# Forming the weight operands of the first two gate/up units earlier, and keeping one unit's operands for both token pairs

## The chip, the cores and the metric

The kernel runs on one NeuronCore of a Trainium2 chip. The core has a matrix engine (TensorE, PE in the profile; its weight loads are the row PEld), VectorE (DVE), ScalarE (ACT), GpSimd (POOL), and SyncE (SP), which issues nearly all DMAs of this kernel, in order. The metric is the device time of one execution in microseconds, smaller is better. Time before is the median of three runs.

## The reference

One layer of a streaming encoder for 1088 tokens (1024 of a prompt, 64 of a running stream) with 1024 channels, all in 32-bit floats. The part that the change touches is the end of the mixer and the start of the feed-forward network:

```python
    x = x + ym @ w_out                      # output projection, 1024 x 1024
    h = rmsnorm(x, g_ffn)
    x = x + (jax.nn.silu(h @ w_gate) * (h @ w_up)) @ w_down      # D_FF = 2816
```

The outputs are the two normalised results and small state tensors.

## The kernel before

**Precision.** A product of 32-bit matrices is made of three passes of TensorE in its rounded 32-bit type: both factors are split into a rounded part (suffix h) and the rest (suffix l), and the passes are h·h, h·l and l·h. ScalarE makes h by a cast, VectorE makes l by a subtraction.

**Gate and up.** The 2816 gate and up columns are worked off in 22 units `j` of 128 gate and 128 up columns (`NF`). The 1088 tokens form two pairs, x = 0 and x = 1, each of two quarters of 272 tokens (`Q`). A unit multiplies a 2x2 block matrix of weights by a 2x2 block matrix of tokens with seven products instead of eight. So there are seven token operands per pair (`R0[c]`, `R1[c]`, named B11, T1, T2, B21, T3, B22, T4 in the order of use, each with h and l) and seven weight operands per unit. A product is 4 (channel tiles) x 3 (passes) = 12 matmuls of 272 columns for one pair, so a unit has 84 matmuls for one pair and 168 for both.

**Weight operands.** `load_w` (L609 to L617) fetches four weight blocks into three slots F (three DMAs on SP). `steps` (L619 on) forms the seven operands in four steps; each step ends in `put`, which takes a slot pair from `w_free`, casts F to h on ScalarE (L627) and subtracts on VectorE (L471). Three pairs hold two operands (128x1024), the fourth holds one (128x512). `fill()` takes steps as long as slot pairs are free; `products` calls it ahead of each product, and gives a pair back (`give`) when both of its operands were used. Slots: F starts with three `raws` tiles; from unit 2 on it has also the tiles R, E and C, ten in all. W has three `ring` pairs, and from unit 2 on a fourth in the tile Hl67.

**PSUM.** A unit adds its seven products up in three accumulators (banks a, b, c) of four buffers. ScalarE copies partial results out (`grab`, L693: p1, p5, u2, u3), VectorE adds (L474) and multiplies (L719, L720) the rest. Bank b is free after the addition of p2 (at B21), bank c after that of p53 (at B22), bank a after the multiplication at T4. The next product into a bank that holds a copied partial result waits for that copy.

**Order of the stages.** The output projection runs over 8 column blocks `m` for x = 0 and then again for x = 1. Its weights, split in the first round, are written to DRAM (`wod`) and reloaded (`reload`) in the second. `out_evac` adds the residual (L474) and ScalarE squares it (L535, L541, L544). After a round come the row sums of squares (`stat`: 1-column matmuls L484, then L489 and POOL's L491), a transposed row (`row`: L497, L498), and `prep(x)`: norms (L574), differences (L471) and the splits (L579, L471) into the seven operands of R0 or R1. `prep(0)` runs during the second round, `prep(1)` after it, among the first units. The list `units` begins (0, x=0), (1, x=0), then units 2 to 5 for both pairs, then (0, x=1), (1, x=1), whose weights are loaded and formed a second time, then the rest.

A scheduler orders the instructions of each engine when the kernel is built; each engine then works through its own list in order.

Of the kernel before, what the change touches and what calls it, by code (L numbers as in the profile page):

```python
# [9 lines left out]
F32 = mybir.dt.float32  # L10
F32R = mybir.dt.float32r
# [3 lines left out]
P = 128  # L15
# [6 lines left out]
HALF = 512  # L22
NF = 22
# [2 lines left out]
EPS = 1e-6  # L26
AHEAD = 2
WARM = 9
EARLY = 3
Q = 272  # L30
CH = ((0, 364), (364, 726), (726, 1088))
XW = HIST + S1 + HIST + S0
# [26 lines left out]
def encoder_kernel(ctx: ExitStack, tc: tile.TileContext, xT, w_in, w_out, w_gu, w_down,  # L59
                   w_spT, w_pool, hist, vec, g_rows, yT, hist_p, hist_s, v_s):  # L60
    nc = tc.nc
    const = ctx.enter_context(tc.tile_pool(name="const", bufs=1))
    big = ctx.enter_context(tc.tile_pool(name="big", bufs=1))
# [3 lines left out]
    dram = ctx.enter_context(tc.tile_pool(name="dram", bufs=1, space=bass.MemoryType.DRAM))  # L67
# [8 lines left out]
    def tmp2():  # L76
        return tmps.tile([P, 2 * Q], F32, tag="t", name="t")
# [334 lines left out]
    Yh = Yl = None  # L412
# [28 lines left out]
    Yh = big.tile([P, 4, T], F32R, tag="Ah", name="Yh")  # L441
    Yl = big.tile([P, 4, T], F32R, tag="Al", name="Yl")
# [27 lines left out]
    def sub(o, a, b):  # L470
        nc.vector.tensor_tensor(out=o, in0=a, in1=b, op=ALU.subtract)  # L471

    def add(o, a, b):
        nc.vector.tensor_tensor(out=o, in0=a, in1=b, op=ALU.add)  # L474
# [43 lines left out]
    def load_x(m, x):  # L518
        t = tmp2()
        nc.sync.dma_start(t, tokens(xT[m], x))  # L520
        return t
# [28 lines left out]
    R1 = []  # L550

    def make_R1():
        h = big.tile([P, 4, 4, Q], F32R, tag="Ah", name="R1h")
        l = big.tile([P, 4, 4, Q], F32R, tag="Al", name="R1l")
        R1.extend((h[:, c], l[:, c]) for c in range(4))
        R1.extend((big.tile([P, 4, Q], F32R, tag=f"B{c}h", name=f"R1h{c + 4}"),
                   big.tile([P, 4, Q], F32R, tag=f"B{c}l", name=f"R1l{c + 4}")) for c in range(3))
# [48 lines left out]
    f_free, w_free = [], []  # L606
    stream_w, loaded, made, left = [], [], [], [0]

    def load_w():  # L609
        while stream_w and len(f_free) >= 3:  # L610
            src, n = stream_w.pop(0)
            slots = [f_free.pop(0) for _ in range(3)]
            F = [slot[:, :, 0:n] for slot in slots]
            nc.sync.dma_start(F[0][:, 0], src[0])
            nc.sync.dma_start(F[2], src[2:4].rearrange("q p c -> p q c"))
            nc.sync.dma_start(F[1][:, 1], src[1])
            loaded.append((F, n, slots))  # L617
# [28 lines left out]
    retired = []  # L646
# [8 lines left out]
    def fill():  # L655
        while w_free and left[0]:
            left[0] -= 1
            next(step)

    def products(n, xs, after, between=None, keep=None, kept=None):  # L660


        x0, x1 = xs[0], xs[-1] + 1
        banks = {}
        for c, b, half, what in ((B11, "a", 0, "p1"), (T1, "c", 1, "p5"), (T2, "a", 0, "u2"), (B21, "b", 1, "p2"),
                                 (T3, "a", 0, "u3"), (B22, "c", 1, "p53"), (T4, "a", 0, "c21")):
            fill()
            wh, wl, slot = (made if kept is None else kept)[0]
            start = b not in banks
            if start:  # L670
                banks[b] = bank2()
            ps = banks[b]
            K = n // P
            for x in xs:
                xh, xl = RR[x][c]
                i = 0
                for k in range(K):
                    for w, v in ((wh, xh), (wh, xl), (wl, xh)):
                        nc.tensor.matmul(ps[:, x, 0:Q], w[:, half, k * P:(k + 1) * P], v[:, k],  # L679
                                         start=start and i == 0, stop=i == 3 * K - 1, skip_group_check=True)  # L680
                        i += 1
            if half or what == "c21":
                if keep is None:
                    give(w_free, [(made if kept is None else kept).pop(0)[2]])
                else:
                    keep.append(made.pop(0))
            after(what, ps[:, x0:x1, 0:Q])
            if between:
                between(c)

    def grab(ps, xs):
        t = tmp2()[:, 0:Q * len(xs)].rearrange("p (x t) -> p x t", t=Q)
        nc.scalar.copy(t, ps)  # L693
        return t
# [3 lines left out]
    G = [None, None]  # L698

    def gu_unit(j, xs, between=None, **how):  # L700
        if j % 2 == 0 and how.get("kept") is None:
            G[:] = [big.tile([P, 2, 2, Q], F32, tag=t, name="G") for t in ("B3h", "B3l")]
        g = G[j % 2]
        g1, g2 = (g[:, n, xs[0]:xs[-1] + 1] for n in range(2))
        s = {}

        def after(what, ps):
            if what in ("p1", "p5", "u2", "u3"):
                s[what] = grab(ps, xs)
            if what == "p2":  # L710
                add(s["p1"], ps, s["p1"])
                nc.scalar.activation(s["p1"], s["p1"], AF.Silu)
            if what == "u3":
                add(s["u3"], s["u3"], s["p5"])
            if what == "p53":
                add(s["u2"], ps, s["u2"])
                nc.scalar.activation(s["u2"], s["u2"], AF.Silu)
            if what == "c21":
                nc.vector.tensor_tensor(out=g1, in0=ps, in1=s["p1"], op=ALU.mult)  # L719
                nc.vector.tensor_tensor(out=g2, in0=s["u3"], in1=s["u2"], op=ALU.mult)  # L720

        products(HALF, xs, after, between, **how)

    def g_operands(p, xs):

        a, e = xs[0], xs[-1] + 1
        G1, G2 = (g[:, :, a:e] for g in G)
        G3 = big.tile([P, 2, 2, Q], F32, tag="sq", name="G3")[:, :, a:e]
        t4 = tmp2().rearrange("p (x t) -> p x t", x=2)[:, a:e]

        def store(c, v, n=2):
            nc.sync.dma_start(gd[p, c:c + n, :, a:e].rearrange("c p x t -> p c x t"), v)

        sub(G3[:, 0], G1[:, 1], G1[:, 0])
        sub(G1[:, 1], G1[:, 1], G2[:, 1])
        store(B11, G1)
        sub(G3[:, 1], G2[:, 1], G3[:, 0])
        store(B21, G2)
        sub(t4, G2[:, 0], G3[:, 1])
        store(T1, G3)  # L740
        store(T4, t4.unsqueeze(1), 1)

    SPLIT, LATER = 2, 6
    units = [(j, (0,)) for j in range(SPLIT)] + [(j, (0, 1)) for j in range(SPLIT, NF)]
    units[LATER:LATER] = [(j, (1,)) for j in range(SPLIT)]
    MP = range(KT // 2)
    downs, base, off = [], 0, 0
    for gi, J in enumerate(GROUPS):
# [1 line left out]
        src = [w_down[off + q * size:off + (q + 1) * size].rearrange("(q p c) -> q p c", q=4, p=P) for q in range(4)]  # L750
        downs.append((base, J, src))
        base, off = base + J, off + 4 * size
    stream_w += [(w_gu[j], HALF) for j, _ in units]
    for _, J, src in downs:
        stream_w += [(src[q], J * P) for q in MP]
    left[0] = 4 * len(stream_w)
# [2 lines left out]
    kept = []  # L759
# [24 lines left out]
    pieces = prep(0)  # L784
    for m in range(KT):
        w = again.pop(0)
        if m + 1 < KT:
            xrs.append(load_x(m + 1, 1))
        ps = w_half(w, 1)
        out_evac(m, 1, xrs.pop(0), ps)  # L790
        next(pieces, None)
        if m + 2 < KT:
            again.append(reload(m + 2))
        if m == 1:
            f_free += [raws.tile([P, 2, HALF], F32, tag="raw", name="F") for _ in range(3)]
            load_w()
        if m >= KT - 3:
            w_free.append((ring.tile([P, 2, HALF], F32R, tag="rh", name="Wh"),
                           ring.tile([P, 2, HALF], F32R, tag="rl", name="Wl")))
            fill()  # L800
    for _ in pieces:
        pass
    make_R1()
    f_free.append(big.tile([P, 2, HALF], F32, tag="R", name="F"))
    pieces = prep(1)


# [9 lines left out]
    def g_next(base, J, x):  # L817

        def between(c):
            g_load(c, base, J, x)  # L820
            g_split(c, J, x)
        return between

    for i, (j, xs) in enumerate(units):
        if i == SPLIT:
            e = big.tile([P, 2, 2, HALF], F32, tag="E", name="F")
            c = big.tile([P, 4, 2, HALF], F32, tag="C", name="F")
            wx = big.tile([P, 2, 2, HALF], F32R, tag="Hl67", name="W")
            extra = [e[:, 0], e[:, 1]] + [c[:, n] for n in range(4)]
            f_free += extra  # L830
            extra_w = (wx[:, 0], wx[:, 1])
            w_free.append(extra_w)
        if i == len(units) - 5:
            retired[:] = [id(slot) for slot in extra]
            give(f_free, [])
        if i < len(units) - 1:
            gu_unit(j, xs, lambda c: next(pieces, None))
        else:
            kept = []
            gu_unit(j, (0,), g_next(0, GROUPS[0], 0), keep=kept)  # L840
            gu_unit(j, (1,), g_next(0, GROUPS[0], 1), kept=kept)
        if j % 2:
            g_operands(j // 2, xs)


# [62 lines left out]
    for gi, (base, J, _) in enumerate(downs):  # L908
# [3 lines left out]
        for q in MP:  # L912
            if 0 < q < MP[-1]:
                down_unit(q, J, (0, 1))
            elif q < MP[-1] or not final:
                kept = []
# [11 lines left out]
    kept, q = [], MP[-1]  # L928
# [70 lines left out]
```

## Time and profile before

| | before |
|---|---|
| median of three runs | 1044.3 us (1043.94, 1044.3, 1048.57) |
| profiled execution, its own time | 1049.64 us |
| its span, first to last instruction | 1047.8 us |
| PE / PEld / DVE / ACT / POOL busy | 1008.5 / 979.5 / 652.0 / 420.9 / 102.9 us |
| instructions on PE | 7355 matmuls |
| mean granted clock of TensorE | 0.976 of full speed |

Busy time counts an instruction from its start to its (for PE modelled) end. The granted clock tells which share of full speed TensorE was allowed; 1.00 is 2.4 GHz and 0.50 is 1.2 GHz. In the view of busy time by stretch a row has the stretch, its length, then for PE, PEld, DVE, ACT and POOL the busy time with the count of instructions, then the granted clock, the mean share of the 16 DMA engines, and GB/s. The views used below are the page's totals, busy time by stretch of time, the waits of one engine, the chain of work that ended last, and instructions in order of time.

### The profile page before, as it was taken

The numbers are of one execution on the slowest core, as the hardware profiler recorded it, in microseconds if no ns is written. First come the engines' busy times: TensorE is split into PE (matmuls) and PEld (weight loads), VectorE is DVE, ScalarE is ACT, GpSimd is POOL, SyncE is SP. The second block draws the span as 40 slices with busy tenths as digits, with TensorE's granted clock in tenths as the row PEclk, the third lists the DMA queues.
The fourth block names the chain that finished last, engine by engine and source line by source line (L and its number), as shares of the span: only waits on it lengthen the run. The fifth ranks groups of instructions, "written<-read, shape, count | busy, mean of one in ns | idle before, by whom it ended". The sixth has DMA issues, their size and how long they took to land.

```text
span 1047.8 us, 17609 instructions
## 1 busy us (share of the span) xinstructions
PE 1008.5 (96%) x7355; PEld 979.5 (93%) x7355; DVE 652.0 (62%) x879; ACT 420.9 (40%) x638; POOL 102.9 (10%) x117
## 2 busy tenths in 40 slices
PE   8999999999979999999999999999989998999995
PEld 6799988999969999999999999999989998999994
DVE  6668728326789556646455545555595578558855
ACT  7373435312353334433333333333473254236530
POOL 6630131111300000000000000000000000000320
PEclk9999999999988999999999999999999999999996
DMA  8211102996604243313314133134584173236104
GB/s 302 71 43 47 62 11 64 377 319 225 224 19 149 61 129 122 119 61 126 117 50 135 51 126 115 41 119 144 173 286 135 44 253 126 77 100 185 53 2 170
DMA packets 71807, 131.83 MB, mean 126 GB/s; under 512 B 7024, under 2 KB 30576, under 8 KB 71728
## 3 DMA queue, kind: packets, MB, share of 16 engines
q1 hardware_dynamic: 70576, 128.49, 37.1%
q10 hardware_dynamic: 1152, 2.23, 0.6%
q8 instruction: 57, 0.93, 0.4%
q14 instruction: 22, 0.18, 0.1%
HBM read 91.75 MB, written 38.94 MB: 125 GB/s over the span
## 4 chain that ended last, share of the span: by engine, by line
PE 81%; DVE 7%; DMA 5%; issue 1%; ACT 1%; SPq 0%; POOL 0%; DVEq 0%; ACTq 0%
PE ps L679 60%; PE ps L95 18%; DMA R1l<-gd 2%; DMA R0l<-gd 1%; PE ps L484 1%; DVE R1l L471 1%; DVE R0l L471 1%; DVE X L574 1%; DMA F<-in_w_gu 1%; DVE Wl L471 1%; DVE accL L474 1%; DVE X L471 1%; DVE X1a L471 0%; DMA t<-in_xT 0%; DMA gd<-G 0%
## 5 line engine op out<-in xcount | busy, mean ns | idle before, releaser
L679 PE MATMUL ps<-R0h,Wh 128*128 128x272 f32 x840 | 246.2, 293 | 7.2 <-DVE t L474 4.4
L679 PE MATMUL ps<-R1h,Wh 128*128 128x272 f32 x832 | 243.0, 292 | 6.2 <-DVE G L719 2.4
L679 PE MATMUL ps<-R0h,Wl 128*128 128x272 f32 x840 | 244.6, 292 | 4.1 <-DVE Wl L471 4.1
L679 PE MATMUL ps<-R0l,Wh 128*128 128x272 f32 x840 | 243.6, 290 | 0.0
L679 PE MATMUL ps<-R1h,Wl 128*128 128x272 f32 x832 | 242.0, 291 | 0.0
L679 PE MATMUL ps<-R1l,Wh 128*128 128x272 f32 x832 | 240.4, 289 | 0.0
L471 DVE TENSOR_TENSOR Wl<-F,Wh 128x1024 fp32r<-128x1024 f32 (+3 forms) x121 | 138.9, 1150 | 103.5 <-ACT Wh L627 103.4
L627 ACT CAST Wh<-F 128x1024 fp32r<-128x1024 f32 (+3 forms) x121 | 118.5, 980 | 207.5 <-PE ps L679 190.1
L679 PEld LDWEIGHTS ps<-R0h,Wh 128*128 128x128 f32 x840 | 159.9, 190 | 9.7 <-DVE t L474 4.8
L679 PEld LDWEIGHTS ps<-R1h,Wh 128*128 128x128 f32 x832 | 157.8, 190 | 8.3 <-ACT t L693 3.5
L679 PEld LDWEIGHTS ps<-R0h,Wl 128*128 128x128 f32 x840 | 159.4, 190 | 5.1 <-DVE Wl L471 4.9
L693 ACT COPY t<-ps 128x544 f32<-128x544 f32 (+1 forms) x172 | 88.2, 516 | 186.4 <-PE ps L679 183.8
L679 PEld LDWEIGHTS ps<-R0l,Wh 128*128 128x128 f32 x840 | 160.3, 191 | 0.0
L679 PEld LDWEIGHTS ps<-R1l,Wh 128*128 128x128 f32 x832 | 157.9, 190 | 0.0
L679 PEld LDWEIGHTS ps<-R1h,Wl 128*128 128x128 f32 x832 | 157.6, 189 | 0.0
L545 POOL TENSOR_TENSOR sq<-sq,t 128x544 f32<-128x544 f32 x20 | 34.8, 1753 | 756.4 <-PE ps L679 679.0
L471 DVE TENSOR_TENSOR F<-F 128x512 f32<-128x512 f32 (+1 forms) x108 | 72.5, 697 | 1.4
L474 DVE TENSOR_TENSOR t<-ps,t 128x544 f32<-128x544 f32 (+1 forms) x50 | 32.6, 652 | 50.0 <-PE ps L679 50.0
L474 DVE TENSOR_TENSOR F<-F 128x512 f32<-128x512 f32 (+1 forms) x36 | 24.3, 675 | 42.0 <-DMA F<-in_w_gu 34.6
L679 PE MATMUL ps<-R0h,W 128*128 128x272 f32 x168 | 36.5, 297 | 2.3 <-ACT t L693 2.3
L679 PE MATMUL ps<-R1h,W 128*128 128x272 f32 x184 | 38.6, 290 | 0.0
L95 PE MATMUL ps<-dh,rh 128*128 128x272 f32 x128 | 37.9, 296 | 0.0
(231 smaller groups left out, 1722.5 us busy)
## 6 DMA issues: line engine op xcount, KB each, us to landing
gd<-G SPq DMA_DIRECT2D x30, 544.0 KB, 4.0
F<-in_w_gu SPq DMA_DIRECT2D x48, 256.0 KB, 2.7
F<-in_w_gu SPq DMA_DIRECT2D x24, 512.0 KB, 3.9
R0l<-gd SPq DMA_DIRECT2D x14, 544.0 KB, 5.3
R1l<-gd SPq DMA_DIRECT2D x14, 544.0 KB, 5.3
raw<-in_w_in SPq DMA_DIRECT2D x11, 512.0 KB, 3.7
t<-in_xT SPq DMA_DIRECT2D x16, 272.0 KB, 4.6
raw<-in_w_out SPq DMA_DIRECT2D x8, 512.0 KB, 5.9
```

Of the source, the lines that this page charges most:

```text
L95: nc.tensor.matmul(ps, a, b, start=first and i == 0, stop=last and i == n - 1)
L471: nc.vector.tensor_tensor(out=o, in0=a, in1=b, op=ALU.subtract)
L474: nc.vector.tensor_tensor(out=o, in0=a, in1=b, op=ALU.add)
L484: nc.tensor.matmul(ps[0:n, i:i + 1], a[:, at + o:at + o + n], ones, start=k == 0, stop=k == len(sums) - 1)
L545: nc.gpsimd.tensor_tensor(out=a, in0=a, in1=t, op=ALU.add)
L574: nc.vector.scalar_tensor_tensor(out=v, in0=v, scalar=g_ffn[:, m:m + 1], in1=pair(R), op0=ALU.mult, op1=ALU.mult)
L627: nc.scalar.copy(h, F[:, 0:k])
L679: nc.tensor.matmul(ps[:, x, 0:Q], w[:, half, k * P:(k + 1) * P], v[:, k], start=start and i == 0, stop=i == 3 * K - 1, skip_group_check=True)
L693: nc.scalar.copy(t, ps)
```

## The change

Four edits. (1) When the first round of the output projection is over, the first 512 tokens of its operand tiles Yh and Yl (tags Ah, Al) are no longer read; two W pairs are laid into them (`once`), used for the first two pairs of unit 0 and never given back. R1's first four operands are from now on views of the same Yh and Yl and no longer new tiles of the tags Ah and Al. (2) `fill()` is called in the second round from its second block on, and the tile R is an F slot from the start. (3) Tile C, free after `prep(0)`, gives two more W pairs (`c_pairs`) until five units before the end, instead of four F slots: F has six slots and W six pairs in the middle of the stage. (4) The list begins (0, x=0), (1, x=0), (1, x=1): unit 1's pairs are kept from one to the other (`keep`, `kept`). Only unit 0's second half, at place 7, loads and forms its weights again. Its partner, unit 1's result for x = 1, waits in DRAM (`gx`) until then. What is computed stays the same.

```diff
@@ make_R1
-        h = big.tile([P, 4, 4, Q], F32R, tag="Ah", name="R1h")
-        l = big.tile([P, 4, 4, Q], F32R, tag="Al", name="R1l")
+        h, l = (t.rearrange("p c (k t) -> p c k t", k=4) for t in (Yh, Yl))
@@ gu_unit
-        if j % 2 == 0 and how.get("kept") is None:
+        if j % 2 == 0 and "kept" not in how:
@@
-    SPLIT, LATER = 2, 6
-    units = [(j, (0,)) for j in range(SPLIT)] + [(j, (0, 1)) for j in range(SPLIT, NF)]
-    units[LATER:LATER] = [(j, (1,)) for j in range(SPLIT)]
+    LATER = 7
+    units = [(0, (0,), 0), (1, (0,), 1), (1, (1,), 2)] + [(j, (0, 1), 0) for j in range(2, NF)]
+    units.insert(LATER, (0, (1,), 0))
@@
-    stream_w += [(w_gu[j], HALF) for j, _ in units]
+    stream_w += [(w_gu[j], HALF) for j, _, how in units if how < 2]
@@ second round of the output projection
-        if m == 1:
+        if m == 0:
             f_free += [raws.tile([P, 2, HALF], F32, tag="raw", name="F") for _ in range(3)]
-            load_w()
+            f_free.append(big.tile([P, 2, HALF], F32, tag="R", name="F"))
+            once = [(Yh[:, k:k + 2, 0:HALF], Yl[:, k:k + 2, 0:HALF]) for k in (0, 2)]
+            retired[:] = [id(slot) for slot in once]
+            w_free += once
+        if m in FILL:
+            fill()
@@
+    wc = big.tile([P, 2, 2, 2, HALF], F32R, tag="C", name="W")
+    c_pairs = [(wc[:, i, 0], wc[:, i, 1]) for i in range(2)]
+    w_free += c_pairs
+    fill()
     make_R1()
-    f_free.append(big.tile([P, 2, HALF], F32, tag="R", name="F"))
@@ loop over the units
-            c = big.tile([P, 4, 2, HALF], F32, tag="C", name="F")
-            extra = [e[:, 0], e[:, 1]] + [c[:, n] for n in range(4)]
+            extra = [e[:, 0], e[:, 1]]
...
-            retired[:] = [id(slot) for slot in extra]
+            retired[:] = [id(slot) for slot in extra + c_pairs]
...
+        if i == LATER:
+            gu_unit(j, xs)
+            nc.sync.dma_start(G[1][:, :, 1], gx)
+            g_operands(0, xs)
+        elif i == 2:
+            gu_unit(j, xs, lambda c: next(pieces, None), kept=kept)
+            nc.sync.dma_start(gx, G[1][:, :, 1])
```

What the change does to the engines' lists shows at two places. The first is VectorE from the copy of the second transposed row (L498) on, that is `prep(1)` among the first units. X1a and X1b are the projection's results, R1l the l parts of R1, t the copied partial results. Before:

```order
L498 COPY t<-ps 128x544
L574 SCALAR_TENSOR_TENSOR X1a<-X1a,vec_sb,t 128x544 x4
L474 TENSOR_TENSOR t<-ps,t 128x272
L574 SCALAR_TENSOR_TENSOR X1b<-X1b,vec_sb,t 128x544 x2
L471 TENSOR_TENSOR R1l<-X1a,R1h 128x1088
L574 SCALAR_TENSOR_TENSOR X1b<-X1b,vec_sb,t 128x544
L471 TENSOR_TENSOR X1a<-X1a 128x4x272
L574 SCALAR_TENSOR_TENSOR X1b<-X1b,vec_sb,t 128x544
L471 TENSOR_TENSOR Wl<-F,Wh 128x1024
L471 TENSOR_TENSOR R1l_2768<-X1a,R1h_2767 128x1088
L471 TENSOR_TENSOR X1a<-X1a,X1b 128x4x272
L471 TENSOR_TENSOR X1a<-X1b,X1a 128x4x272
```

After (Yl is here the l part of an R1 operand, W a pair in tile C):

```order
L498 COPY t<-ps 128x544
L471 TENSOR_TENSOR W<-F,W 128x1024
L573 SCALAR_TENSOR_TENSOR X1a<-X1a,vec_sb,t 128x544 x4
L474 TENSOR_TENSOR t<-ps,t 128x272
L573 SCALAR_TENSOR_TENSOR X1b<-X1b,vec_sb,t 128x544 x2
L471 TENSOR_TENSOR Yl<-X1a,Yh 128x1088
L573 SCALAR_TENSOR_TENSOR X1b<-X1b,vec_sb,t 128x544
L471 TENSOR_TENSOR X1a<-X1a 128x4x272
L573 SCALAR_TENSOR_TENSOR X1b<-X1b,vec_sb,t 128x544
L474 TENSOR_TENSOR t<-t 128x272
L471 TENSOR_TENSOR X1a<-X1a,X1b 128x4x272
L471 TENSOR_TENSOR R1l_2783<-X1a,R1h_2782 128x1088
```

One weight subtraction stands ahead of the norms, where before the first stood among the splits. Further down, the list before has three more Wl of unit 1 during or right behind the splits; the list after has there unit 1's last and smallest one (128x512) and unit 2's first.

The second place is ScalarE at the same time, from the copies of unit 0's first partial results (COPY t) on; CAST Wh and CAST W are weights, the other casts are R1's h parts. Before:

```order
L693 COPY t<-ps 128x272 x3
L627 CAST Wh<-F 128x1024
L579 CAST R1h<-X1a 128x1088
L712 ACT_TABLE_LOAD
L712 ACTIVATE t<-t 128x272
L693 COPY t<-ps 128x272
L627 CAST Wh<-F 128x1024
L579 CAST R1h_2767<-X1a 128x1088
```

After:

```order
L692 COPY t<-ps 128x272 x2
L626 CAST W<-F 128x1024
L692 COPY t<-ps 128x272
L626 CAST Wh<-F 128x512
L578 CAST Yh<-X1a 128x1088
L711 ACT_TABLE_LOAD
L711 ACTIVATE t<-t 128x272
L692 COPY t<-ps 128x272
L578 CAST R1h_2782<-X1a 128x1088
L578 CAST Yh<-X1b 128x1088 x2
L578 CAST Yh<-X1a 128x1088
L692 COPY t<-ps 128x272 x2
```

A weight cast stands ahead of R1's first cast in both lists. Before it is unit 1's first pair, into the slots of unit 0's second pair; after it is unit 1's last pair, into the slots of unit 0's third pair, which TensorE reads until the product B22 of unit 0. The copies of unit 1's p1 and p5 stand behind all four casts into Yh.

## Rows read from the trace of the kernel before

**Rows 1.** The page: busy time (share of the span) x instructions of each engine.

```profile
PE 1008.5 (96%) x7355; PEld 979.5 (93%) x7355; DVE 652.0 (62%) x879; ACT 420.9 (40%) x638; POOL 102.9 (10%) x117
```

**Rows 2.** Busy time by stretch, four stretches.

```profile
60.00:236.00 176.00, 176.00 (x1111) 165.08 (x1109) 99.79 (x143) 71.46 (x130) 31.46 (x45) 1.00 0.39 137
284.00:296.00 12.00, 11.03 (x68) 10.58 (x67) 5.39 (x10) 2.22 (x5) 2.56 (x2) 0.72 0.21 68
296.00:324.00 28.00, 19.67 (x124) 18.48 (x124) 27.45 (x35) 16.49 (x23) 0.00 (x0) 0.82 0.18 58
324.00:756.00 432.00, 432.00 (x3427) 431.85 (x3426) 242.66 (x328) 156.34 (x218) 0.00 (x0) 1.00 0.32 105
```

**Rows 3.** Waits of PE from 284 to 324: us in total, times, longest.

```profile
PE ps L679 <- DVE Wl L471: 4.1, 2, 2.7
PE ps L679 <- DVE t L474: 3.7, 1, 3.7
PE ps L484 <- ACT t L535: 1.0, 1, 1.0
PE ps L679 <- ACT t L693: 0.5, 1, 0.5
```

**Rows 4.** Chain of work that ended last, 278 to 326: start, us, what.

```profile
285.02 0.73 DVE X1b L474
...
286.48 4.43 PE ps L484 x26
...
294.45 0.74 DVE t L498
...
295.21 2.48 DVE X1a L574 x4
...
299.82 1.20 DVE R1l L471
301.02 0.70 DVE X1b L574
...
303.61 1.14 DVE Wl L471
...
311.11 0.35 DVE t L474
```

**Rows 5.** Busy time in stretches of 5 us, columns as in rows 2.

```profile
240.00:245.00 5.00, 5.00 (x33) 5.00 (x32) 0.00 (x0) 0.00 (x0) 0.71 (x2) 0.74 0.48 186
310.00:315.00 5.00, 0.82 (x2) 0.51 (x2) 5.00 (x6) 1.53 (x2) 0.00 (x0) 0.59 0.00 0
315.00:320.00 5.00, 4.95 (x22) 4.95 (x23) 5.00 (x7) 1.42 (x2) 0.00 (x0) 0.50 0.17 24
320.00:325.00 5.00, 4.93 (x35) 4.72 (x35) 4.30 (x9) 2.52 (x5) 0.00 (x0) 0.89 0.98 358
```

**Rows 6.** PE in order of time: start, us, what [idle before <- releaser].

```profile
311.51 0.59 PE L679 MATMUL ps<-R0h,Wh 128*128 128x272 f32 x1 [3.68 <-DVE t L474]
```

**Rows 7.** DVE in order of time.

```profile
284.41 0.69 DVE L474 TENSOR_TENSOR F<-F 128x512 f32<-128x512 f32 x1 [3.71 <-DMA F<-in_w_gu]
...
326.28 0.43 DVE L719 TENSOR_TENSOR G<-ps,t 128x272 f32<-128x272 f32 x1
```

**Rows 8.** ACT in order of time.

```profile
283.34 1.05 ACT L627 CAST Wh<-F 128x1024 fp32r<-128x1024 f32 x1 [3.01 <-PE ps L95]
...
297.54 1.05 ACT L627 CAST Wh<-F 128x1024 fp32r<-128x1024 f32 x1 [0.94 <-PE ps L679]
...
299.61 1.28 ACT L712 ACT_TABLE_LOAD   x1
...
301.24 0.37 ACT L693 COPY t<-ps 128x272 f32<-128x272 f32 x1
```

**Rows 9.** SP's queue in order of time.

```profile
246.53 0.32 SPq L769 DMA_DIRECT2D rh<-wod  x1
```

**Rows 10.** VectorE's groups from 324 to 756, one group (busy us, mean ns, idle before).

```profile
L474 DVE TENSOR_TENSOR F<-F 128x512 f32<-128x512 f32 x21 | 14.5, 691 | 28.6 <-DMA F<-in_w_gu 26.8 <-DMA F<-in_w_down 1.7
```

More of the change, by code (lines that the diff above doesn't have):

```diff
@@ L28 @@
 WARM = 9
-EARLY = 3
+FILL = range(1, 8)
 Q = 272
@@ L822, in g_next @@
         return between
-    for i, (j, xs) in enumerate(units):
-        if i == SPLIT:
+    gx = dram.tile([P, 2, Q], F32, name="gx")
+    kept = []
+    for i, (j, xs, how) in enumerate(units):
+        if i == 3:
+            for _ in pieces:
+                pass
             e = big.tile([P, 2, 2, HALF], F32, tag="E", name="F")
-            c = big.tile([P, 4, 2, HALF], F32, tag="C", name="F")
             wx = big.tile([P, 2, 2, HALF], F32R, tag="Hl67", name="W")
-            extra = [e[:, 0], e[:, 1]] + [c[:, n] for n in range(4)]
+            extra = [e[:, 0], e[:, 1]]
             f_free += extra
@@ L833, in encoder_kernel @@
         if i == len(units) - 5:
-            retired[:] = [id(slot) for slot in extra]
+            retired[:] = [id(slot) for slot in extra + c_pairs]
             give(f_free, [])
-        if i < len(units) - 1:
-            gu_unit(j, xs, lambda c: next(pieces, None))
+        if i == LATER:
[5 more added lines that the diff above has]
+            nc.sync.dma_start(gx, G[1][:, :, 1])
+        elif i < len(units) - 1:
+            gu_unit(j, xs, lambda c: next(pieces, None), **(dict(keep=kept) if how else {}))
         else:
@@ L841, in encoder_kernel @@
             gu_unit(j, (1,), g_next(0, GROUPS[0], 1), kept=kept)
-        if j % 2:
+        if j % 2 and how < 2:
             g_operands(j // 2, xs)
```

## Prediction

> **What bounds the kernel now.** The page's totals [rows 1] say TensorE, at 96% busy, but an average hides where time can be won. So I went to busy time by stretch [rows 2]. From 60 to 236 and from 324 to 756 PE is busy without a gap at clock 1.00: 3427 matmuls in 432 us are 0.126 us each, and nothing that other engines save there can show. From 284 to 324, the stretch between the output projection and full speed in the units, PE has 68 + 124 = 192 instructions in 40 us. At 0.126 they would take 24.2 us, so about 15.8 us are lost, partly as idle time (12 - 11.03 + 28 - 19.67 = 9.3 us), partly because the clock stood at 0.72 and 0.82. In the second part of it VectorE is busy 27.45 of 28 us. The waits of PE [rows 3] name what it stood for: weights (Wl, 4.1 us), an addition that frees a PSUM bank (t, 3.7 us), small ones. The chain of work [rows 4] runs through VectorE for nearly all of 294 to 317: norms, splits of R1 and weight subtractions share one queue. The stretches of 5 us [rows 5] show the price of standing still: after the 3.68 us wait that ends at 311.51 [rows 6] the clock is 0.50 from 315 to 320 (1.2 GHz; 22 matmuls in 5 us, 0.227 each) and 0.89 in the next 5 us.
>
> Later stretches with lost time (the down projection's operands, the end) are not touched by the change, so this one stretch decides.
>
> **The change, part by part.** *Weights of unit 0 in Yh and Yl.* Two casts and about five VectorE operations move into the time from 230 to 246. VectorE is idle from 240 to 245 [rows 5], PE needs none of them before 284: cost 0. The loads stand where they stood, except that unit 1's 512 KB load now goes ahead of a weight reload on SP. That reload waited for PE until 246.53 anyway [rows 9], and by then the load, which waits for a subtraction at about 240, is long issued. If it were late, the reload and then the projection would be late by as much.
>
> *The second stat.* Its last square waits for the addition of block 7, which stood at 285.02 behind an F addition that waited for a load until 284.41 [rows 4, 7]. TensorE had finished that block at about 283.3 (ScalarE's cast waited for it until 283.34, [rows 8]). In the new order weight subtractions stand ahead of it whose loads are issued near 275 and land before 280. So the addition comes at 283.4, 1.4 us earlier (with its square and the sums behind it, 285.1 instead of 286.48). The end of the sums, which I call S, was 286.48 + 4.43 = 290.9 and becomes 289.5. Bounds: 0 earlier, if the casts ahead of the square are in the way, to 2.8, if the clock should not fall during the sums.
>
> *The units behind it.* All pairs of unit 0 and the first two of unit 1 are ready by S, so the waits for Wl (4.1 us) go. What is late next is found by walking the new lists with the durations of the old trace: a matmul 0.126, a split or difference of 1088 elements 1.20, a norm 0.70, a weight subtraction 1.14, an addition 0.35 [rows 2, 4]; a cast 1.05, the table load 1.28 and a copy 0.37 on ScalarE [rows 8]. Times from S:
> - The copy of the row ended at 295.19, S + 4.3 [rows 4], and does so again. VectorE: the weight subtraction now ahead (1.14), four norms (2.48), p2 (0.35), two norms (1.4): S + 9.7.
> - Its next operation needs R1's first cast. In ScalarE's list that stands behind a cast into the pair that PE reads until unit 0's B22. PE begins T2 at S + 3.5; four products, 48 matmuls, are 6.0, so S + 9.5. Then the two casts, 0.6 and 1.05: VectorE goes on at S + 11.2, 1.5 us late. The same kind of wait was 0.94 before [rows 8].
> - VectorE: one split, two norms, three differences, two more splits, one addition, in all 1.2 + 1.4 + 3.6 + 2.4 + 0.35 = 8.95, to S + 20.2; then p53's addition, S + 20.55. It frees the bank for unit 1's B21.
> - PE meanwhile: unit 1's B11, then T4 of unit 0, which waits for the copy of u3 behind the table load (11.2 + 1.28 + 0.35 + 0.37 = 13.2), idle some 1.6; the rest of T1 to 15.7; T2 waits for the copy of p1 that stands behind the four R1 casts, S + 18.9, idle 3.2; B21 waits for p53 at 20.55. B21 and B22 end at 23.6.
> - Unit 1's second pair needs bank a of unit 0, which the multiplication behind two splits, a weight of half size (0.6) and a difference frees: 20.55 + 4.2 + 0.35 = 25.1, idle 1.5. Then 24 matmuls, and T4 after its copy: 30.25. VectorE's p2 of unit 1, behind two splits, 0.95 of unit 2's weights and products and its first Wl, is done at 29.95 and holds nothing up.
> So at S + 30.25 = 319.75 PE has done 168 matmuls of units 0 and 1 and 12 of unit 1's second pair, and from there has work without a gap. Before, the 168 ended with unit 1's T4 at about 326.2 (its multiplication starts at 326.28, [rows 7]), so 180 would stand at 327.7. Gain 8.0.
>
> *The clock.* The idle 3.2 us is of the length of the 3.68 [rows 6], after which PE ran half speed until near 320.8, about 5.7 us after its last wait (315 to 320 at 0.50, 0.89 in the next 5, [rows 5]). Here 5.7 us at 0.227 cover 25 matmuls, where 45 were possible; most is hidden by the 1.5 us wait for bank a, some 0.4 is left. With half clock for 9.3 us, all the time from 311.5 to 320.8, 1.9 are left. I take 1.0.
>
> *One unit's weights less* (about 6.4 us of VectorE, 3.7 of ScalarE) lies from 400 on beside a PE without gaps: nothing. The way of a result through DRAM is covered by unit 0's 84 matmuls, 10.6 us; uncovered it would hold VectorE for one load. From five units before the end the slots are as many as before.
>
> Sum: 1.4 + 6.6 (what the walk gives with S unmoved, 327.7 - 290.9 - 30.25) - 1.0 = 7.0. The profiled execution would go from 1049.64 (span 1047.8 and 1.84 around it) to 1042.6. The median is 5.3 lower than that execution; I take the same 7.0 off it: **1037.3 us**. Own bounds: without the earlier S, with 1.9 for the clock and 2 for waits that my walk doesn't see, 2.7; with S 2.8 earlier and no clock loss, 9.4.
>
> **A rule on headroom.** The weight-load row is busy 10.58 + 18.48 of these 40 us [rows 2], so 10.9 of it are not. The Trainium skill (Perfetto Trace Analysis, Identifying the Most-Contended Engine) holds the busy share of weight loads, and not that of matmuls, to be the measure of TensorE's headroom. By it no more than 10.9 could be won here, by the matmuls' own idle time 9.3, by my count 15.8. The trace speaks for the count, since loads at half clock count as busy as well (4.95 of 5 us with 23 of them at 0.50, [rows 5]).
>
> **Rivals.** *The whole loss goes.* If ScalarE and VectorE kept PE fed from S on, only the sums would stay, some 4 of the 15.8: 1044.3 - 11.8 = 1032.5. For it: weights were the largest wait. Against: unit 1's second pair now needs R1 about 10 us earlier in PE's order, and VectorE has some 21 us of work for it. Chance 0.06.
>
> *The waits only change their names.* Bank and copy waits stay (p53 came at 311.11 before, [rows 4], and by the walk comes at 310), the half clock lasts longer, and the gain is 1 to 5, about 3: 1041.3. For it: VectorE was busy 27.45 of 28 us and loses only three weight subtractions there; each queue works in order. Against: by the walk only three waits are left, 6.3 us, and the clock has room behind the third. Chance 0.24.
>
> *Slower, by the steady units.* F has six slots instead of ten, so each load is issued later; VectorE, which already stood 26.8 us for 21 loads from 324 to 756 without harm [rows 10], would stand longer with additions behind it that free banks. VectorE is idle 189 of 432 us there, some 9 per unit; if loads came later than that and PE lost 0.6 us in each of 19 units, that is 11.4, less 7.0 is +4.4; with 0.7, +6.3: 1050. It decides from about 0.65 us per unit on. Against: six W pairs instead of four form weights further ahead. Chance 0.08.
>
> **How the numbers follow.** 0.5% is 5.2 us, about what a measurement of this kernel can tell from no change. My forecast, a gain over that, has 0.62, with its own range 1034.5 to 1039; with the first rival, faster is 0.68. The second rival makes same 0.24, the third slower 0.08. The range from 1032 to 1043 holds my case, most of the second and the edge of the first.
>
> **What would show it.** Right: the second sums end 1 to 3 us earlier; between 284 and 324 no wait of PE for Wl, but waits for copies (t on ScalarE) and for p53's addition, together 5 to 7 us; the bank wait still ends near 310; about 240 PE instructions instead of 192 between 284 and 324; VectorE with 8 instructions less; from 324 on no gap until the down projection. Wrong: gaps among the steady units, a late reload after 246, or PE at half clock beyond 320.

## The result, and the profile after the change

| | before | after |
|---|---|---|
| median, same chip | 1044.44 us (1043.94 to 1048.57) | 1037.3 us (1034.83 to 1038.9) |
| ratio, 95% interval | | 0.9909 (0.989 to 0.9928) |
| profiled execution | 1049.64 us, span 1047.8 | 1037.52 us, span 1035.7 |

The change made the kernel faster, by 7.1 us in the medians and by 7.5 to 11.5 us in the interval of the ratio, 9.5 us at its estimate. The median is the one predicted, to the tenth, and that is luck: the four runs of each kernel spread by over 4 us, and the steps behind the time are only partly the ones predicted. Two runs of the experiments below took far longer than the rest (2370.62 us in "changed", 1697.52 us in less_vector), and the medians below leave them out.

The page's first line after, columns as in [rows 1]:

```profile
PE 1004.0 (97%) x7355; PEld 976.4 (94%) x7355; DVE 649.2 (63%) x871; ACT 415.5 (40%) x634; POOL 102.8 (10%) x117
```

Busy time by stretch, columns as in [rows 2]:

```profile
284.00:296.00 12.00, 12.00 (x90) 11.79 (x89) 7.05 (x11) 3.53 (x6) 1.90 (x2) 0.86 0.26 84
296.00:324.00 28.00, 24.88 (x173) 24.30 (x172) 27.52 (x40) 15.45 (x23) 0.00 (x0) 0.88 0.24 76
324.00:746.00 422.00, 422.00 (x3345) 421.62 (x3344) 233.50 (x310) 147.38 (x208) 0.00 (x0) 1.00 0.32 105
...
305.00:310.00 5.00, 3.79 (x16) 3.79 (x17) 5.00 (x6) 2.87 (x5) 0.00 (x0) 0.53 0.01 3
310.00:315.00 5.00, 5.00 (x33) 5.00 (x33) 5.00 (x8) 1.69 (x3) 0.00 (x0) 0.78 0.19 52
```

From 284 to 324 TensorE has 263 instructions instead of 192. At 0.126 us they take 33.1 of the 40 us: 6.9 us are lost instead of 15.8, 3.1 as idle time and 3.7 to half clock (36.88 busy less 33.1). VectorE is still busy 27.52 of 28 us. Behind 324 there is no gap.

TensorE's waits from 284 to 324 [rows 3], and the chain of work [rows 4]:

```profile
PE ps L678 <- ACT t L692: 3.1, 1, 3.1
```

```profile
285.99 2.40 PE ps L484 x26
288.39 2.79 PE ps L678 x11
...
292.26 0.35 DVE t L498
...
301.78 1.11 ACT R1h L578
...
306.21 19.90 PE ps L678 x133
```

Five waits of four kinds have become one. VectorE and ScalarE in order of time, in one fence each:

```profile
283.94 0.72 DVE L474 TENSOR_TENSOR X1b<-ps,t 128x544 f32<-128x544 f32 x1 [1.90 <-PE ps L95]
...
307.51 0.44 DVE L474 TENSOR_TENSOR t<-ps,t 128x272 f32<-128x272 f32 x1
...
312.06 0.45 DVE L718 TENSOR_TENSOR G<-ps,t 128x272 f32<-128x272 f32 x1
```

```profile
296.74 0.62 ACT L626 CAST Wh<-F 128x512 fp32r<-128x512 f32 x1 [2.46 <-PE ps L678]
...
300.01 0.37 ACT L692 COPY t<-ps 128x272 f32<-128x272 f32 x1
...
304.78 1.09 ACT L578 CAST Yh<-X1a 128x1088 fp32r<-128x1088 f32 x1
305.78 0.66 ACT L692 COPY t<-ps 128x272 f32<-128x272 f32 x2
```

How much of the gain arises here? The last multiplication of the gate and up units (line of G) shows it, first before, then after:

```profile
779.51 0.43 DVE L719 TENSOR_TENSOR G<-ps,t 128x272 f32<-128x272 f32 x1
```

```profile
771.44 0.44 DVE L718 TENSOR_TENSOR G<-ps,t 128x272 f32<-128x272 f32 x1
```

8.1 us are won by then. The two spans differ by 12.1; the other 4 us lie in the down projection, which the change leaves alone: from that row to the end it took 268.3 us in this execution of before, 264.3 after, and 264.7 in an experiment below that leaves all of before's work as it was. They belong to the one execution.

### The profile page after: what moved, and what is told of

Its sections match the earlier page's. It is cut to its first block, busy times and chain, and to the rows that moved or that the text cites. A ratio compares the mean times of both kernels' runs of the same rounds, so it can differ in the third digit from the quotient of the medians.

```text
span 1035.7 us, 17622 instructions
## 1 busy us (share of the span) xinstructions
PE 1004.0 (97%) x7355; PEld 976.4 (94%) x7355; DVE 649.2 (63%) x871; ACT 415.5 (40%) x634; POOL 102.8 (10%) x117
## 4 chain that ended last, share of the span: by engine, by line
PE 87%; DVE 4%; DMA 2%; issue 1%; ACT 1%; POOL 0%; DVEq 0%; ACTq 0%
PE ps L678 63%; PE ps L95 21%; DMA R0l<-gd 1%; PE ps L484 1%; DVE Yl L471 0%; DMA R1l<-gd 0%; DVE R1l L471 0%; DVE accL L474 0%; PE ps L497 0%; PE ps L418 0%; DVE X1a L573 0%; DVE Wl L471 0%; PE ps L141 0%; ACT Yh L578 0%; ACT t L692 0%
## 5 line engine op out<-in xcount | busy, mean ns | idle before, releaser
L471 DVE TENSOR_TENSOR Wl<-F,Wh 128x1024 fp32r<-128x1024 f32 (+2 forms) x96 | 102.8, 1073 | 77.6 <-ACT Wh L626 77.6
L678 PE MATMUL ps<-R0h,W 128*128 128x272 f32 x568 | 121.2, 294 | 3.1 <-ACT t L692 3.1
L678 PE MATMUL ps<-Yh,Wh 128*128 128x272 f32 x352 | 102.6, 292 | 4.0 <-DVE G L718 2.2
L678 PE MATMUL ps<-Yh,Wl 128*128 128x272 f32 x352 | 102.2, 290 | 0.0
L678 PE MATMUL ps<-Yl,Wh 128*128 128x272 f32 x352 | 101.7, 289 | 0.0
L678 PEld LDWEIGHTS ps<-R0h,W 128*128 128x128 f32 x568 | 95.5, 193 | 3.5 <-ACT t L692 3.5
L678 PE MATMUL ps<-R1h,Wh 128*128 128x272 f32 x280 | 82.1, 293 | 1.0 <-ACT t L692 1.0
L678 PE MATMUL ps<-R0l,W 128*128 128x272 f32 x284 | 83.0, 292 | 0.0
L678 PE MATMUL ps<-R1h,Wl 128*128 128x272 f32 x280 | 81.6, 292 | 0.0
L678 PE MATMUL ps<-R1l,Wh 128*128 128x272 f32 x280 | 81.1, 290 | 0.0
```

## The experiments

All were timed beside the kernel before on their own chip. Since the median of before differs from one set of runs to the next (1045.95 to 1048.34, both on one chip), the ratios are compared. "G" is the start of the last gate/up multiplication in the profile; starts of the stretch differ by up to 1.6 us between executions (the addition of block 7 starts at 282.83 in bank_first and at 284.39 in early_bank). Before, G is 779.51 and the waits are 9.3 us; after, 771.44 and 3.1.

| | median | ratio (95%) | G | waits of TensorE, 284 to 332 |
|---|---|---|---|---|
| early_alone | 1036.54 | 0.9905 (0.9885 to 0.9926) | 770.60 | 3.5 |
| keep_alone | 1041.85 | 0.9945 (0.9926 to 0.9965) | 774.74 | 7.6 |
| unit0_alone | 1041.73 | 0.9954 (0.9934 to 0.9974) | 773.74 | 7.1 |
| copy_first | 1037.07 | 0.9904 (0.9879 to 0.9928) | 770.80 | 4.5 |
| bank_first | 1037.79 | 0.9916 (0.9892 to 0.994) | 770.34 | 5.2 |
| early_bank | 1038.78 | 0.9911 (0.9886 to 0.9936) | 772.74 | 5.1 |
| before_bank | 1046.82 | 1.0 (0.9983 to 1.0016) | 779.33 | 11.1 |
| f4 | 1035.49 | 0.9889 (0.9868 to 0.9909) | 769.62 | 3.3 |
| changed | 1037.23 | 0.9913 (0.9896 to 0.993) | 772.04 | 3.1 |
| evac_first | 1036.66 | 0.9907 (0.9888 to 0.9927) | 769.62 | 3.3 |
| casts_pool_evac | 1041.08 | 0.9956 (0.9937 to 0.9975) | 774.75 | 8.2 |
| less_vector | 1031.33 | 0.9849 (0.9823 to 0.9875) | 766.40 | 1.2 |

### Which part of the change gains

**early_alone.** The list of units, and the weights formed twice, as before:

```diff
-    units = [(0, (0,), 0), (1, (0,), 1), (1, (1,), 2)] + [(j, (0, 1), 0) for j in range(2, NF)]
-    units.insert(LATER, (0, (1,), 0))
+    units = [(j, (0,), 0) for j in range(SPLIT)] + [(j, (0, 1), 0) for j in range(SPLIT, NF)]
+    units[LATER:LATER] = [(j, (1,), 0) for j in range(SPLIT)]
...
```

> The early formation without keeping: unit 0's pairs in Yh and Yl, the two pairs in tile C, the earlier fill, but the list of units of the kernel before (0 and 1 for x = 0, then 2 to 5 for both pairs, then 0 and 1 for x = 1 with their weights loaded and formed again). Theory 1, early formation is the whole gain and keeping unit 1 pays nothing, because what it saves (one unit's weights) lies beside a TensorE without gaps: 1037 to 1039 us, the same gain as the full change within 2 us. Theory 2, the kept unit is needed as cover, since its 84 matmuls (10.6 us) ask for no new weights while VectorE finishes R1: without it TensorE waits for unit 2's weights from about 316 on, 1040 to 1043 us. In the trace: a wait of TensorE for Wl or W between 316 and 330 speaks for 2, none for 1.

The same ratio as the whole change. TensorE has the same wait, and unit 2's weights cost it 0.4 us, for a cast:

```profile
PE ps L678 <- ACT t L692: 3.1, 1, 3.1
PE ps L678 <- ACT Wh L626: 0.4, 1, 0.4
```

Theory 1 holds: keeping unit 1 adds nothing that can be measured to the early formation (each interval is some 4 us wide).

**keep_alone.** Yh and Yl get no weights, the second round is as before; tile C still gives its two pairs ahead of `prep(1)`, and unit 1 is kept:

```diff
...
-            once = [(Yh[:, k:k + 2, 0:HALF], Yl[:, k:k + 2, 0:HALF]) for k in (0, 2)]
...
-            w_free += once
-        if m in FILL:
-            fill()
+            load_w()
...
```

> Keeping without the early formation: the list of units of the changed kernel, unit 1's pairs kept, tile C as two pairs, but nothing laid into Yh and Yl, and the loads and forming in the second round as before. Theory 1 (early formation is the gain): VectorE has some 4 us more of weights among the norms and splits, so p53's addition and the multiplications come 3 to 4 us later than in the changed kernel; about half of the gain or less, 1040 to 1043 us. Theory 2 (keeping, or the pairs in tile C, bring the gain by themselves): 1037 to 1039 us.

A good half of the gain (0.55% of 0.91%), in the range of theory 1. At G it is 4.8 us, and 2.6 of these are there when the row sums end (288.3 here, 290.9 before; how far the clock has a part in that, the account below says), so that keeping unit 1 and tile C's pairs bring some 2 us behind them. Weights stand again among the norms and splits, and R1's casts, which the copy of p1 stands behind, come later: TensorE waits 7.6 us for it, until 310.52.

```profile
PE ps L677 <- ACT t L691: 7.6, 1, 7.6
```

**unit0_alone.** Tile C again holds F slots, and the list is that of before:

```diff
-    wc = big.tile([P, 2, 2, 2, HALF], F32R, tag="C", name="W")
-    c_pairs = [(wc[:, i, 0], wc[:, i, 1]) for i in range(2)]
-    w_free += c_pairs
-    fill()
...
```

> Only unit 0's first two pairs formed early; tile C gives F slots as before, no unit is kept, the list is that of before. Unit 1's pairs are then formed into slots that unit 0 gives back, in the middle of R1's splits. Theory 1 (what counts is that both units are ready when the sums end): TensorE waits for Wl of unit 1 near 310, about 3 to 4 us later than the copy it waits for in the changed kernel: 1040 to 1042 us. Rival (unit 0's pairs alone are the gain, for instance by the earlier second sums): 1037 to 1038.5 us. The end of the second sums shows apart what they give: 2.5 us earlier in the changed kernel than before.

Theory 1 again: behind the copy comes a second wait, for unit 1's weights, up to 310.60.

```profile
PE ps L678 <- ACT t L692: 3.2, 1, 3.2
PE ps L678 <- DVE Wl L471: 2.7, 1, 2.7
```

So neither half of the early pairs is enough; both units must be ready when the sums end.

### What bounds it now

**copy_first, bank_first.** The changed kernel with single instructions put first on their engine as soon as they are ready: the copy of unit 1's p1; or unit 0's p53 addition and its multiplication out of bank a.

```diff
-                s[what] = grab(ps, xs)
+                if (j, what, xs) == (1, "p1", (0,)):
+                    with tc.high_priority():
+                        s[what] = grab(ps, xs)
...
-                add(s["u2"], ps, s["u2"])
+                if (j, xs) == (0, (0,)):
+                    with tc.high_priority():
+                        add(s["u2"], ps, s["u2"])
...
```

> The changed kernel with one instruction of ScalarE moved: the copy of unit 1's first p1 (x = 0) goes ahead of three of R1's casts instead of behind four. In the changed kernel TensorE's only wait between 284 and 324 ends with that copy (3.1 us, at 306.2), and half clock follows it. Theory A, that copy is the bound: the wait and the half clock behind it go, 1031 to 1034 us. Theory B, VectorE's list is the bound, p53's addition at 307.5 to 307.9 and the multiplication that frees bank a at 312.4 come as late as ever: TensorE waits 3 us for the addition instead, then half clock again, second pair of unit 1 at 313 as now: 1036.3 to 1037.5 us.

> The changed kernel with two of VectorE's instructions moved forward: unit 0's p53 addition ahead of R1's first split (in the changed kernel at 307.5, though TensorE's product was done near 296.7), and the multiplication that frees unit 0's bank a behind R1's first difference (there at 312.1); the copy of unit 1's p1 comes forward with them on ScalarE. Nothing is added or left out. Theory B (TensorE's loss after the sums is the place of these instructions in the lists, and not the amount of VectorE's work): the waits for the copy, the addition and bank a all go, with the half clock behind them; unit 1's second pair begins near 307 instead of 313.5, and R1's operands come just in time for it: 1030.5 to 1032.5 us. Rival: VectorE's 21 us of work for R1 is the bound, TensorE waits for an R1 split instead, near 308 to 316: 1035 to 1037 us.

copy_first did in the main what theory B said: the time stays, and TensorE now waits for VectorE, though for the multiplication that frees bank a and not for the addition; 1.5 us of waiting for a copy are left.

```profile
PE ps L678 <- DVE G L722: 2.8, 1, 2.8
PE ps L678 <- ACT t L692: 1.5, 1, 1.5
```

But bank_first speaks against B. The three waits went, unit 1's second pair could begin without them, and nothing was won: TensorE ran on to 308.4 and there waited for the next copy, which stands behind R1's last cast, and that for a difference of VectorE.

```profile
PE ps L678 <- ACT t L692: 3.7, 1, 3.7
PE ps L678 <- DVE t L474: 1.3, 1, 1.3
```

It is not one of R1's splits, as the rival had it; the time, 1037.79, is 0.8 us above the rival's range and over 5 above that of B.

**early_bank, before_bank.** The edit of bank_first, in early_alone and in the kernel before.

> The same two instructions moved forward in the kernel with early formation alone (no unit kept). TensorE then reaches unit 2 near 311, but VectorE has unit 2's first weights only behind all of R1's splits, near 317. If a kept unit is worth what it covers, TensorE waits some 5 us for unit 2's Wl and the time stays at 1035.5 to 1037.5 us, 4 to 6 us over the kernel with both. If keeping is worth nothing here either: 1030.5 to 1032.5 us, like the kernel with both.

> The same two instructions moved forward in the kernel before. If the order of these two was the main loss there too, its 3.7 us wait and the half clock behind it go: 1038 to 1041 us where before has 1044.4. If unit 1's weights bind (they stand among R1's splits; the third pair's subtraction ends near S + 24.4 = 315.3, where TensorE waited for it until 315.05 before), the wait only changes its name to Wl: 1043 to 1045 us.

early_bank gains nothing on early_alone; TensorE waits 5.1 us, but for a copy that ends at 314.7, and not for unit 2's weights, so this run doesn't tell what the kept unit is worth. In before_bank the addition came at 299.6 instead of 311.03, and its wait turned into waits for weights: one of 5.8 us that ends at 308.14, and three of 0.5 to 1.1 behind it. Without early weights the order of these two is worth nothing.

```profile
PE ps L679 <- DVE Wl L471: 7.4, 3, 5.8
PE ps L484 <- ACT t L535: 2.1, 1, 2.1
PE ps L679 <- ACT Wh L627: 1.1, 1, 1.1
```

**changed, evac_first.** The changed kernel again; and with every instruction that empties a bank of units 0 and 1 (x = 0) put first:

```diff
+        def early(what, ps):
+            with tc.high_priority():
+                after(what, ps)
...
-        products(HALF, xs, after, between, **how)
+        products(HALF, xs, early if j < 2 and xs == (0,) else after, between, **how)
```

> The changed kernel itself once more, so that the two versions of this call can be set against it on one chip. Its interval so far is 0.989 to 0.9928 of the time before; the same again, near 0.991. The profile tells whether the half clock behind the row sums, which three of the kernels so far did not show (clock 1.00 from 284 to 296), comes and goes with one and the same program.

> The changed kernel with every copy, addition and multiplication that empties a PSUM bank of units 0 and 1 (x = 0) put first on its engine wherever it is ready; nothing added or left out. Theory B (places in the lists): TensorE runs from the sums to unit 1's second pair near 309 without a wait, R1's operands come just in time, and T4 of that pair ends some 33 us behind the sums instead of 35.7: 1033.5 to 1035.5 us, 2.5 to 3.5 less than the changed kernel. Rival (the wait only moves on): the copies of the second pair's p1 and p5 stand on ScalarE behind R1's last cast and two casts of unit 2's weights, which wait for VectorE's addition behind R1's splits; TensorE waits 3 to 5 us for them, until about 316, with half clock behind it: 1036.5 to 1039 us.

TensorE now runs without a wait from the sums to 313.5. Then it waits for weights, the last of unit 1 (128x512) and the first of unit 2, which VectorE and ScalarE have only among and behind R1's last splits:

```profile
PE ps L678 <- DVE Wl L471: 1.9, 2, 1.1
PE ps L678 <- ACT Wh L626: 1.4, 1, 1.4
```

G is 2.4 us earlier than in "changed", the time 0.6 us lower, and the intervals overlap: this gain is not shown. The wait moved on, as my rival had it, and the time is in the rival's range; but it moved to weights, and the second pair's copies, which the rival named, were no wait.

**casts_pool_evac.** As evac_first, with R1's casts on GpSimd; what empties the banks of unit 1 for x = 1 is put first as well, so it differs from evac_first in two things.

```diff
-            nc.scalar.copy(h, v)
+            if x:
+                nc.gpsimd.tensor_copy(h, v)
+            else:
+                nc.scalar.copy(h, v)
...
-        products(HALF, xs, after, between, **how)
+        products(HALF, xs, early if j < 2 and (j, xs) != (0, (1,)) else after, between, **how)
```

> As the one before, and R1's seven casts are made by GpSimd, which does nothing from 296 to 950 otherwise, so that no copy of ScalarE stands behind a cast that waits for VectorE's differences. No row shows a cast on GpSimd; its addition of 128x544 takes 1.75 us, so I put a cast of 128x1088 between 1.7 and 3.5. If it is under 2: 1033.5 to 1036 us, the copy waits of units 0 and 1 gone, the one behind unit 2's weight casts still there. If it is nearer 3, or slows VectorE beside it: VectorE waits for casts, splits come late, 1037 to 1041 us.

A cast takes 1.3 to 2.15 us, and yet the time is that of the bad case: VectorE is slowed beside it (shown in the last section), and gets through 28 instructions from 296 to 324 where it does 39 in evac_first (whose row stands under less_vector).

```profile
296.00:324.00 28.00, 20.04 (x137) 18.80 (x137) 27.08 (x28) 3.77 (x8) 11.82 (x7) 0.87 0.08 23
```

**less_vector.** As evac_first, without two of VectorE's 1.2 us differences for R1. What it leaves out the layer needs, so this kernel serves for its time only:

```diff
-        sub(b12, b12, b22)
+        if not x:
+            sub(b12, b12, b22)
...
-        sub(b11, b21, b11)
+        if not x:
+            sub(b11, b21, b11)
```

> The kernel with the copies, additions and multiplications first, and two of VectorE's three differences of 1088 elements for R1 left out (the operands T3 and T4 of the second token pair are then the undiffered blocks; the rest is unchanged): 2.4 us less work of VectorE between the sums and unit 2's first weights, in the same order. In the kernel with them TensorE's waits after the sums all end with weights that stand behind R1's splits on VectorE (0.8 at 314.4, 1.4 at 317.2, 1.1 at 318.9), and half clock follows the last. Theory C, what is left of the loss is VectorE's amount of work, whatever the order: these waits go, unit 2 starts 2 to 3 us earlier, the last multiplication of the gate/up units starts near 767 instead of 769.6, and the time is 1032.5 to 1034.5 us. Rival, something else is late at the same time (loads, slots): 1036 to 1037 us, with waits of the same length under another name.

Theory C holds. One wait of 1.2 us is left, the clock is 1.00 from 296 on, TensorE has 209 instructions there instead of 181, and G is 3.2 us earlier; its interval lies below that of evac_first. VectorE comes to unit 2's first subtraction at 315.22 instead of 317.57, earlier by the 2.4 us of work that it is spared.

```profile
296.00:324.00 28.00, 26.78 (x209) 26.17 (x207) 27.07 (x39) 16.11 (x26) 0.00 (x0) 1.00 0.28 91
...
PE ps L680 <- DVE Wl L471: 1.2, 1, 1.2
```

The same row of evac_first:

```profile
296.00:324.00 28.00, 24.73 (x181) 24.08 (x180) 27.86 (x39) 14.19 (x22) 0.00 (x0) 0.94 0.23 74
```

### The rival that ended slower

**f4.** The changed kernel with four F slots instead of six:

```diff
-            extra = [e[:, 0], e[:, 1]]
-            f_free += extra
+            extra = []
```

> The changed kernel without the two F slots in tile E: four F slots instead of six (ten in the kernel before), so that never more than one unit's load is under way. My rival of the prediction: fewer slots make loads later, VectorE waits for them, and from 0.65 us of lost time per unit on the change turns to a loss; then this kernel, with a load issued only when the one ahead of it is used up, is slower than the changed one by 6 us or more. If TensorE has enough cover (six W pairs formed ahead, VectorE idle 9 us per unit): within 1.5 us of the changed kernel, 1036 to 1039 us, with more idle time of VectorE before F additions and no wait of TensorE from 324 to 746.

It is not slower. VectorE's additions stood longer for loads from 324 to 746 (first the changed kernel, then f4), and TensorE had no gap there.

```profile
L474 DVE TENSOR_TENSOR F<-F 128x512 f32<-128x512 f32 x21 | 14.5, 691 | 25.6 <-DMA F<-in_w_gu 23.8 <-DMA F<-in_w_down 1.8
```

```profile
L474 DVE TENSOR_TENSOR F<-F 128x512 f32<-128x512 f32 x21 | 14.5, 690 | 33.2 <-DMA F<-in_w_gu 31.5 <-DMA F<-in_w_down 1.8
...
324.00:746.00 422.00, 422.00 (x3345) 421.62 (x3344) 231.82 (x309) 147.37 (x207) 0.00 (x0) 1.00 0.32 106
```

## Why the prediction was right

Count to the same piece of work, 180 matmuls of units 0 and 1. After, the 181st starts at 318.26. Before, unit 1's T4 begins at 323.61 and its 168th matmul is over by 325.22, where unit 2 begins; 12 more end at 326.92:

```profile
318.26 0.29 PE L678 MATMUL ps<-R1h,Wh 128*128 128x272 f32 x1
```

```profile
323.61 0.39 PE L679 MATMUL ps<-R0h,Wh 128*128 128x272 f32 x1
...
325.22 0.29 PE L679 MATMUL ps<-R0h,Wh 128*128 128x272 f32 x1
...
326.92 0.29 PE L679 MATMUL ps<-R0l,Wh 128*128 128x272 f32 x1
```

That is 8.7 us, of which 8.1 are left at G. My 7.0 was made of three terms, each wrong by about 1 us:

- **The earlier sums: 1.4 predicted, 2.5 measured** (290.9 to 288.39). The order did what was predicted: block 7's addition comes right behind TensorE, at 283.94 instead of 285.02, and the 0.97 us pause ahead of the 26 sums is gone. By itself this makes the sums begin only 0.5 us earlier in these profiles (285.99 instead of 286.48), because in the profile of after TensorE was also 0.5 us later with block 7 (its first matmul of unit 0 is at 283.74 instead of 283.26). The other 2.0 us are the length of the sums, 2.40 us instead of 4.43 [rows 4], which were mostly at half clock before (0.50 from 287 to 291). I had taken this as a bound only, "if the clock should not fall during the sums". It is not shown to come from the change: in before_bank, whose lists are those of before up to there, a longer pause stands ahead of the sums, and they still take only 2.7 us (286.76 to 289.49). In keep_alone, with the addition at 283.74, they take 2.53. So up to 2 us of the 8.7 are the clock of these two executions.

```profile
286.76 0.38 PE L484 MATMUL ps<-ones,t 128*128 128x1 f32 x2 [2.09 <-ACT t L535]
...
289.49 0.59 PE L679 MATMUL ps<-R0l,Wh 128*128 128x272 f32 x1
```

```profile
285.78 2.53 PE ps L483 x26
```

- **The row that I set it against: 0.8 too far.** I took the multiplication at 326.28 [rows 7] as the end of unit 1's T4. VectorE got to it more than 1 us late, behind a weight; the 180 matmuls of before ended at 326.9 and not at 327.7.
- **The walk: S + 31.25 with the clock's 1.0, measured S + 29.9.** Of its four waits one came as predicted: PE stood 3.12 us for p1's copy (predicted 3.2, S + 18.9; measured S + 17.8). VectorE's wait of 1.5 us was not there: I let the weight cast wait for unit 0's B22, as the part on the change says as well, but it is of half size and writes only the half of the slot that T3 reads, and so began at S + 8.35. With it, the 1.6 us wait for u3's copy fell away (300.01, in time). The additions for B21 and bank a came about when predicted (S + 19.5 and S + 24.0, each 1.1 earlier), but TensorE, at half clock from 306.21 to about 312, was not there before them. The half clock itself was as long as predicted (5.8 us, 25 matmuls) and cost 2.7 us. I had taken 1.0 for it beside the waits (the 0.4 behind that is 0.9 by its own rows); here its whole cost counted, and it hid the two waits.

7.0 + 1.1 - 0.8 + 1.4 is 8.7, so the three do not cancel; the 7.1 between the medians is nearer to 7.0 than the stretch is. What was right: the stretch, the waits for weights gone, VectorE's 8 instructions less, no cost from 324 on. What was wrong in its list of signs: 3.1 us of waits instead of 5 to 7, none of them for p53's addition or for bank a, and 263 instructions instead of about 240.

Of the rivals, "the waits only change their names" is not what this change did, but it is what every further change of order did (copy_first, bank_first, early_bank): VectorE is busy 26 to 27.9 of the 28 us from 296 on in all of them, and as long as its work stands between the sums and the next weights, the wait moves to whichever consumer comes next. less_vector shows the amount to be the bound. "The whole loss goes" failed on that. "Slower, by the steady units" failed in the changed kernel, where TensorE has no gap from 324 to 746, and in f4, with four slots.

Part (4) of the change, keeping unit 1, was costed at nothing in the steady units; early_alone agrees, within its interval. Whether it would pay with less work on VectorE was not tried.

The prediction had three measures of what this stretch could give at most: 9.3 us by the idle time of the matmuls, 10.9 by that of the weight loads, 15.8 by the count of matmuls at full speed. The change, with 8.7, does not tell them apart, but less_vector does. With the same 7355 matmuls its G is 13.1 us earlier than that of before (766.40 and 779.51, one execution each), more than the first two measures allow.

## What to carry to other kernels

When a stretch is bound by one engine's amount of work, moving single instructions to the front renames the wait and leaves the time; moving work out of the stretch, to where that engine has idle time beside a busy TensorE, is what gains, and it must cover all that the next consumer needs. Count from the work itself (the n-th matmul), not from the instruction of another engine that follows it. And look at which part of a tile an instruction writes before you let it wait for the tile's last reader. And before a gain in one profile is put down to the change, look whether another execution of the old lists has it too, as before_bank has the short sums.

## What the hardware showed that was not expected

**GpSimd beside VectorE.** In casts_pool_evac GpSimd's casts (first fence) lengthen VectorE's instructions (second fence) with both inputs in SBUF: a split of 1088 elements takes 2.17 us instead of 1.29, an addition of 272 takes 1.33 instead of 0.43, while an addition with one input in PSUM keeps 0.43 (at 306.51, beside the two casts that run from 303.42 to 307.54).

```profile
303.42 4.12 POOL L579 CAST Yh<-X1b 128x1088 fp32r<-128x1088 f32 x2 [0.71 <-DVE X1b L573]
307.49 2.15 POOL L579 CAST Yh<-X1a 128x1088 fp32r<-128x1088 f32 x1
309.58 1.30 POOL L579 CAST R1h<-X1a 128x1088 fp32r<-128x1088 f32 x1
```

```profile
306.51 0.43 DVE L474 TENSOR_TENSOR t<-ps,t 128x272 f32<-128x272 f32 x1
...
308.60 1.33 DVE L474 TENSOR_TENSOR t<-t 128x272 f32<-128x272 f32 x1
309.85 2.17 DVE L471 TENSOR_TENSOR Yl<-X1b,Yh 128x1088 fp32r<-128x1088 f32 x1
```

The addition that starts at 308.60 ends 0.3 us behind the cast's end (309.64), the split that starts at 309.85 ends 1.1 us behind the next cast's end (310.88): each seems to have stood until GpSimd was done. The Trainium skill (SBUF — State Buffer, Who interferes with whom and Summary: rules for kernel authors) says that a VectorE instruction with two SBUF inputs contends with a GpSimd instruction that reads SBUF, and that the second of the two to issue is blocked until the first has finished; these rows agree.

**Half clock behind the row sums comes and goes.** The changed kernel's lists are the same up to there in "changed" and in f4. In the one TensorE ran at half clock from 288 to beyond 294, in the other not at all; the first execution of the changed kernel stands between them (0.86).

```profile
284.00:296.00 12.00, 12.00 (x79) 11.67 (x78) 6.55 (x11) 3.04 (x6) 1.90 (x2) 0.72 0.28 83
```

```profile
284.00:296.00 12.00, 11.84 (x100) 11.42 (x99) 8.21 (x14) 3.94 (x8) 1.90 (x2) 1.00 0.29 91
```

That is 21 matmuls, 2.6 us, between executions that were given the same instructions up to there; the four runs of the changed kernel spread by 4.1 us (1034.83 to 1038.9). The sums of before (4.43 us) and of before_bank (2.7) show the same for the lists of before. What decides it was not settled.
